# A fused two-mixer decoder layer: norm diagonals in a row, a doubling moved ahead, GELU's argument copied out of PSUM, and k gains applied behind the transposition

## The chip, the cores and the metric

The kernel runs on one core of one Trainium2 chip, as one launch. The metric is the device time of that launch in microseconds (us), the median of several runs. Inputs and outputs are float32.

The engines are named as in the profile: PE (TensorE, matmuls), DVE (VectorE), ACT (ScalarE), POOL (GpSimd) and SP (SyncE, which issues most DMAs). Every engine runs its instructions in the order in which they stand in the program; semaphores hold an instruction back until its operands are there and its buffer is free.

## The reference, cut to what matters

The layer takes x (1 x 512 x 1024), norms it, multiplies it by one wide input weight, and feeds two attention mixers of eight heads with 64 channels each. Mixer A (MoBA) is block-sparse attention; with 512 tokens and blocks of 256 its selection keeps every past block. Mixer B (NSA) has three branches: k and v compressed by a small MLP, selected blocks, and a window, the k of each branch with a gain vector of its own. The two outputs are gated, projected, merged and projected again.

```python
def rms_norm(x, g):
    y = xf * lax.rsqrt(jnp.mean(xf * xf, axis=-1, keepdims=True) + EPS)
    return y * g

def compress(kv, pos, w1, w2):          # windows of 32 tokens, stride 16
    win = kv[:, idx] + pos ...
    return jax.nn.gelu(win @ w1) @ w2

h = rms_norm(x, norm_w)
proj = h @ w_in
(q_a, k_a, v_a, z_a, q_b, kc, vc, ksl, vsl, kwn, vwn, gate_b, z_b, gate_m) = split(proj)
o_a = moba_mixer(rms_norm(q_a, q_norm_a), rms_norm(k_a, k_norm_a), v_a, bias_a)
k_cmp = rms_norm(compress(kc, ...), k_norm_cmp);  v_cmp = compress(vc, ...)
o_b = nsa_mixer(rms_norm(q_b, q_norm_b), k_cmp, v_cmp,
                rms_norm(ksl, k_norm_sel), vsl, rms_norm(kwn, k_norm_win), vwn, gate_b, bias_b)
merged = sigmoid(..) * ((o_a * silu(z_a)) @ w_branch_a) + sigmoid(..) * ((o_b * silu(z_b)) @ w_branch_b)
return x + merged @ w_out
```

## The kernel before, in words

**Float32 from three matmuls.** A float32 operand is split into a high part (rounded to fp32r) and a low part (the rest, again fp32r), and a product is hi·hi + lo·hi + hi·lo, all into one PSUM tile (`mm3`, L386). For a weight tile `wr` (128 x 512, from DRAM), ACT or POOL writes the high part `wh` (L352, L356) and DVE the low part `wl` (L361). A product over 1024 rows has eight such k tiles.

**A planner inside the kernel.** The kernel text holds streams of work (attention A, projections, compression, the norm of x) that yield to one another, and chains of small vector work. A chain's step is queued with `Chain.do(cost, f)`, where the cost names the engines that may do it and its length there in ns. While the program is built, the planner replays a modelled time `now`: it pops the chain step that is due first, puts it on the engine where it would end first, and books the cost. So the costs fix, at build time, the static order of each engine, and nothing is decided on the chip. A `do` whose function issues nothing still books its cost.

**Buffers.** PSUM tiles come from four groups: "g" (2 tiles, projections), "s" (2, scores), "t" (3, transpositions and small products), "o" (1, outputs). An instruction that writes a tile waits for the last reader of the tile that had the buffer before.

**The norm of x.** `rx` (128 x 4) is 1/rms for each token, token t·128 + p at (p, t). POOL makes it with a power (L513). It is used per token as a scale on copies out of PSUM (L718), and per column of a transposed product as a row R, the same in every partition. R is made on PE: `x_diag` (L519 to L531) splits `rx` into `rxh` (L523, POOL) and `rxl` (L524, DVE), multiplies the identity matrix with each (`dg`, L528, 128 x 512), and `x_rows` multiplies ones with the two `dg` into `prx` (L541). In this time PE runs the k tiles of `pgt` and `pgf`, projections; DVE also has the `v` tiles (L775) in its queue.

**q and k.** A projection of four heads comes out with tokens in partitions (`pgt`). `norm` (L709) copies it to `nraw` with the scale `rx` (L718, ACT), squares it (L720, ACT, with the later output tile as scratch), sums per head (L721, DVE), takes the power (POOL) and multiplies (L723). The gain vectors lie in `gn`, 6 x 64 floats repeated in all partitions; `norm` multiplies by q's and k's gain together where it can, on k alone. For mixer B's k, called `kb` (two groups with selected and window k each, 256 columns), that is L729, on DVE or POOL. `k_pair` (L969) then transposes 128 columns of four token tiles on PE into one PSUM tile `pq` (64 channels of one head in partitions 0 to 63, of the next in 64 to 127), and makes for each of the two heads `ks` (the high part twice, in partitions 0 to 63 and 64 to 127; L978, ACT) and `kx` (the low part in partitions 0 to 63, L980, DVE, and doubled into 64 to 127, L983, ACT). Mixer B's also leave `kf`, copies of the first 128 columns (L989). `q_pair` does the same for q: high part on top, low part below (`qs`, L963, L965).

**Attention.** A unit is one head. `qk` issues two matmuls per 128 queries into a score tile `sps`: `qs` with `ks` (L1024) and with `kx` (L1025). DVE adds the bias and finds the minimum in one custom instruction (`sb`, L1043, the last reader of `sps`), ACT exponentiates (L1058), POOL divides by the sum (L1062), PE transposes (`pt`, L1071), ACT and DVE split the result (`ph`, `pl`, L1083, L1085), and PE multiplies by v (L1105). `moba_units` has a `k_pair` for every second head, h = 0, 2, 4, 6, and `nsa_units` has two for `kb`.

**Compression.** `compress_h` (L852) multiplies windows with w1 into PSUM, copies the result to `hs` (L868, ACT), transposes it on PE into a PSUM tile `pu` (L873), and applies GELU in its tanh form: square on ACT (L878), times 0.044715 plus 1 on DVE (L879), times u on DVE (L880, u read from PSUM), tanh on ACT (L881), plus 1 and times u on DVE (L882, the last reader of `pu`). It runs once for k and once for v.

Of the kernel before, what the change touches and what calls it, by code (L numbers as in the profile page):

```python
# [106 lines left out]
def hybrid_kernel(ctx: ExitStack, tc: tile.TileContext, x, x0, xT, wtok, wchan, wz, wgate, gains, w1,  # L107
# [411 lines left out]
    def x_diag(c):  # L519
# [3 lines left out]
        c.do({"p": 160}, lambda e: e.tensor_scalar(rh, rx, 1.0, 1.0, op0=ALU.mult, op1=ALU.mult))  # L523
        c.do({"D": 70}, lambda e: e.tensor_sub(rl, rx, rh.bitcast(F32)))  # L524
        for r in (rh.bitcast(F32), rl):
            d = att("dg")
            dg.append(d)
            c.do(either(512), lambda e, r=r, d=d: e.tensor_mul(  # L528
                d.rearrange("p (t c) -> p t c", t=NT), ident.unsqueeze(1).to_broadcast([P, NT, P]),
                r.unsqueeze(2).to_broadcast([P, NT, P])))  # L530
# [178 lines left out]
    def norm(ch, dst, ps, t, H, gi):  # L709
# [14 lines left out]
        if gi == 1:  # L724
            z = out[:, 4:]
            ch.do(either(256), lambda e: e.tensor_mul(z, z, gn[:, 1, :].unsqueeze(1).to_broadcast([P, 4, DH])))
        elif gi:
# [1 line left out]
            ch.do(either(256), lambda e: e.tensor_mul(z, z, gn[:, gi:gi + 2, :].unsqueeze(2).to_broadcast([P, 2, 2, DH])))  # L729
# [120 lines left out]
    def compress_h(kv):  # L850
# [27 lines left out]
        ch.do({"A": 160}, lambda e: e.activation(t1, u, AF.Square))  # L878
# [90 lines left out]
    def k_pair(boxes, name, col, firsts=None):  # L969
# [5 lines left out]
        kk = [(att("ks"), att("kx")) for _ in range(2)]  # L975
        for r, (ks, kx) in enumerate(kk):
            for i in range(2):
                c.do({"A": 478}, lambda e, r=r, z=ks[64 * i:64 * i + 64, :]: e.copy(z, pt[64 * r:64 * r + 64, :]))  # L978
        for r, (ks, kx) in enumerate(kk):
            c.do({"D": 602}, lambda e, r=r, ks=ks, kx=kx: e.tensor_sub(  # L980
                kx[0:64, :], pt[64 * r:64 * r + 64, :], ks[0:64, :].bitcast(F32)), pt if r else None)
# [852 lines left out]
```

## Time and profile before

| | |
|---|---|
| median of 3 runs | 451.82 us (451.51 to 451.89) |
| the profiled execution's own time | 450.7 us |
| its span, first to last instruction | 448.9 us |
| granted TensorE clock, mean over the span | 0.999 |
| PE, busy | 441.9 us |
| DVE, busy | 383.2 us |
| ACT, busy | 302.8 us |
| POOL, busy | 199.9 us |

The span is 1.8 us shorter than the time of the same execution (450.7 − 448.9). Times in the profile count from the start of the span. In a row of a timeline the first number is the start, the second the duration, then come the engine, the line of the kernel, the operation and its tiles (out <- in) with their shapes; "x2" says that two like instructions in a row are taken together, and a bracket gives the idle time of the engine just before and who ended it. A row of the groups gives the count, then the busy time in all, the mean of one in ns, and behind a second bar the idle time before and its releaser. In a row of the waits stand who waited, for whom, the time in all, how many waits, and the longest.

### The profile page before, as it was taken

What the parts mean: (1) busy time and instruction counts of PE and PEld (TensorE: products, weight loads), DVE (VectorE), ACT (ScalarE), POOL (GpSimd) and SP (SyncE); (2) the same over time, 40 slices, a digit from 0 to 9 for tenths busy, and PEclk for the clock granted to TensorE, in tenths of its full rate; (3) what the DMA queues carried; (4) which work ended last, traced back from release to release, by engine and by line L of the source; (5) the groups of instructions that cost most, each with busy time, mean ns of one, the idle gap of its engine ahead of it and who ended that gap; (6) DMA issues with size and microseconds to landing.
All of it is one profiled execution on the core that took longest, in us unless ns stands there. A gap on an engine that the chain in (4) does not pass through costs nothing.

```text
span 448.9 us, 8538 instructions
## 1 busy us (share of the span) xinstructions
PE 441.9 (98%) x2779; PEld 394.0 (88%) x2779; DVE 383.2 (85%) x937; ACT 302.8 (67%) x711; POOL 199.9 (45%) x235
## 2 busy tenths in 40 slices
PE   8999999999999999999999999999999999999997
PEld 7878888899778999888999999989988999998886
DVE  5999899889997797788899899977967699899773
ACT  6866678867988798376877777687764355464450
POOL 1242337866685573177675654663770222211000
PEclk9999999999999999999999999999999999999999
DMA  8984655887975969859987867986667888889872
GB/s 252 300 269 166 245 157 180 206 244 197 265 200 164 216 208 279 287 142 220 245 239 203 220 189 170 249 221 159 194 179 174 241 227 249 243 239 295 283 235 95
DMA packets 55085, 98.21 MB, mean 219 GB/s; under 512 B 5312, under 2 KB 9536, under 8 KB 55040
## 3 DMA queue, kind: packets, MB, share of 16 engines
q1 hardware_dynamic: 39808, 68.30, 47.3%
q0 software_dynamic: 7616, 14.68, 20.3%
q10 hardware_dynamic: 7616, 14.68, 9.8%
q8 instruction: 22, 0.36, 0.3%
q14 instruction: 23, 0.19, 0.1%
HBM read 90.69 MB, written 36.31 MB: 283 GB/s over the span
## 4 chain that ended last, share of the span: by engine, by line
PE 79%; DVE 9%; ACT 7%; issue 2%; DMA 2%; POOL 0%; SPq 0%; ACTq 0%; DVEq 0%
PE pgw L386 19%; PE pgt L386 14%; PE pbr L386 10%; PE po L386 9%; PE pgc L386 7%; PE O L1105 6%; PE pt L1071 5%; PE sps L1024 3%; PE sps L1025 3%; DMA wr<-in_wtok 2%; DVE wl L361 1%; ACT ks L978 1%; DVE sb L1043 1%; DVE pl L1085 1%; PE pq L947 1%
## 5 line engine op out<-in xcount | busy, mean ns | idle before, releaser
L361 DVE TENSOR_TENSOR wl<-wr,wh 128x512 fp32r<-128x512 f32 (+1 forms) x150 | 103.5, 708 | 2.7 <-ACT wh L352 2.3
L352 ACT CAST wh<-wr 128x512 fp32r<-128x512 f32 (+1 forms) x130 | 76.7, 608 | 15.0 <-DMA wr<-wsum 6.5
L356 POOL TENSOR_SCALAR wh<-wr 128x512 fp32r<-128x512 f32 (+1 forms) x39 | 30.6, 794 | 79.2 <-DVE wl L361 20.9
L1062 POOL TENSOR_SCALAR P<-P,sst,gate 128x512 f32<-128x512 f32 (+3 forms) x56 | 46.7, 837 | 39.3 <-DVE sst L1061 31.3
L1058 ACT ACTIVATE P<-sb,sst 128x512 f32<-128x512 f32 (+3 forms) x88 | 50.7, 577 | 16.0 <-DVE sst L1043 14.6
L1043 DVE CUSTOM_DVE_ANT_0 sb<-sps,T 128x512 f32<-128x512 f32 (+3 forms) x96 | 46.0, 483 | 13.8 <-PE sps L1025 12.7
L386 PE MATMUL pgt<-wh,hh 128*128 128x512 f32 (+2 forms) x160 | 56.6, 354 | 0.0
L386 PE MATMUL pgt<-wl,hh 128*128 128x512 f32 (+2 forms) x160 | 55.9, 349 | 0.0
L386 PE MATMUL pgt<-wh,hl 128*128 128x512 f32 (+2 forms) x160 | 55.7, 348 | 0.0
L386 PE MATMUL pgw<-th,wh 128*128 128x256 f32 x240 | 48.8, 280 | 0.2 <-DVE gm L1519 0.2
L1083 ACT CAST ph<-pt 128x512 fp32r<-128x512 f32 (+2 forms) x72 | 33.8, 476 | 19.6 <-PE pt L1071 18.5
L386 PE MATMUL pgw<-hh,wh 128*128 128x256 f32 x160 | 45.1, 282 | 0.2 <-ACT c L1460 0.2
L386 PE MATMUL pgw<-hh,wl 128*128 128x256 f32 x160 | 44.4, 277 | 0.0
L386 PE MATMUL pgw<-hl,wh 128*128 128x256 f32 x160 | 44.4, 277 | 0.0
L1071 PE MATMUL pt<-cst,P 128*128 128x128 f32 x232 | 40.7, 272 | 0.3 <-DVE pl L1085 0.3
L1085 DVE TENSOR_TENSOR pl<-pt,ph 128x512 fp32r<-128x512 f32 (+2 forms) x72 | 38.7, 549 | 2.0 <-ACT ph L1083 1.8
L386 PEld LDWEIGHTS pgw<-th,wh 128*128 128x128 f32 x240 | 39.4, 188 | 0.8 <-DVE gm L1519 0.4
L427 POOL TENSOR_TENSOR nr<-nss,mhalf 128x8 f32<-128x8 f32 (+1 forms) x16 | 26.6, 1664 | 22.1 <-DVE nss L426 20.6
L386 PEld LDWEIGHTS pgt<-wl,hh 128*128 128x128 f32 x160 | 30.1, 188 | 4.4 <-DVE wl L361 0.4
L386 PE MATMUL pgw<-th,wl 128*128 128x256 f32 x120 | 33.3, 278 | 0.0
L386 PEld LDWEIGHTS pgt<-wh,hh 128*128 128x128 f32 x160 | 30.1, 188 | 3.4 <-ACT nraw L718 0.2
L386 PEld LDWEIGHTS pgt<-wh,hl 128*128 128x128 f32 x160 | 30.1, 188 | 3.3
(271 smaller groups left out, 1289.6 us busy)
## 6 DMA issues: line engine op xcount, KB each, us to landing
wr<-wsum SPq DMA_DIRECT2D x56, 256.0 KB, 3.8
wr<-in_wtok SPq DMA_DIRECT2D x36, 256.0 KB, 4.8
wsum<-in_wgate ACTq DMA_DIRECT2D x16, 512.0 KB, 5.3
wsum<-wsum POOLq DMA_DIRECT2D x14, 512.0 KB, 7.6
wr<-in_wgate SPq DMA_DIRECT2D x24, 256.0 KB, 4.8
xsum<-th SPq DMA_DIRECT2D x16, 256.0 KB, 2.4
T<-rtab SPq DMA_DIRECT2D x16, 256.0 KB, 5.3
wr<-in_w SPq DMA_DIRECT2D x16, 256.0 KB, 4.6
```

What stands on the lines that cost most here:

```text
L352: e.copy(hi, raw)
L356: e.tensor_scalar(hi, raw, 1.0, 1.0, op0=ALU.mult, op1=ALU.mult)
L361: c.do({"D": cd(n)} if lead else either(n), lambda e, hi=hi, lo=lo, raw=raw: e.tensor_sub(lo, raw, hi.bitcast(F32))).mark((w, 1, i))
L386: nc.tensor.matmul(dst, sts[i][a], mvs[i][b], start=(start and i == a == b == 0), stop=(stop and i == n - 1 and b == 1), skip_group_check= ...
L427: c.do({"p": 430 + POWC * w}, lambda e: e.tensor_tensor(v(dst), v(ss), mhalf[:parts, :w], op=ALU.pow))
L1043: e.tensor_tensor_reduce(z["sb"][:, :L], sps[:, :L], T[:, S - L:], scale=-1.0, scalar=3e38, op0=ALU.add, op1=ALU.min, accum_out=st[:, 0, b ...
L1058: e.activation(pv(), z["sb"][:, :L], AF.Exp, bias=st[:, 0, b:b + 1], scale=-1.0, accum_out=st[:, 1, b:b + 1])
L1062: c.do({"P": 315 + 0.834 * L}, lambda e: e.tensor_scalar(pv(), pv(), st[:, 2, b:b + 1], g, op0=ALU.mult, op1=ALU.mult))
L1071: nc.tensor.transpose(pt[:, (b - kb) * P:(b - kb + 1) * P], u.p0 if u.p0 is not None and b == 0 else u.pb[:, POFF[b] + kb * P:POFF[b] + (k ...
L1083: e.copy(z["w"][0], pt[:, :w])
L1085: ch.do({"D": cd(w)}, lambda e: e.tensor_sub(z["w"][1], pt[:, :w], z["w"][0].bitcast(F32)), pt)
L1105: nc.tensor.matmul(O[0][:, S - n:], v.bitcast(F32) if kb == 3 else v, w, start=(u.first and kb == 0 and i == 0), stop=(u.last and kb == 3 ...
```

## The change

Four edits; what PE computes, and the order of PE and of SP, are as before.

1. **Diagonals in a row.** In `x_diag`, `rxh` is a copy on DVE in place of a step on POOL, right ahead of `rxl`, and both `dg` multiplies are issued one behind the other. The costs that are no longer needed stay booked, with steps that issue nothing.
2. **k of mixer B weighted behind its transposition.** `norm` issues no gain multiply for `kb` (its cost stays booked). In `k_pair` for `kb` the four `ks` copies of a pair are an ACT activation Copy with a column of gains as scale, and the low part of `kx` is, on DVE, pq times the column minus `ks`. The columns (`gcol`: channel in partitions, one column per gain vector, the 64 channels twice) lie in the freed space of `gn`, whose array on the host is 128 x 262 in place of 384 floats; two of the four gain steps in `load_consts` work on 128 x 1 in place of 128 x 64.
3. **A doubling sooner.** In the `k_pair` of heads 4 and 5 of mixer A (h == 4), the doubling of the first `kx` is queued at once when its low part has been issued, not behind the low part of the second.
4. **GELU's argument copied.** In `compress_h`, ACT copies u from PSUM to SBUF right behind the square; the two steps in the middle go from DVE to POOL and read the copy, as does the last step on DVE.

```diff
@@ constants
+    gcol = gn[:, 4, :6]
@@ x_diag
-        c.do({"p": 160}, lambda e: e.tensor_scalar(rh, rx, 1.0, 1.0, op0=ALU.mult, op1=ALU.mult))
-        c.do({"D": 70}, lambda e: e.tensor_sub(rl, rx, rh.bitcast(F32)))
-        for r in (rh.bitcast(F32), rl):
...
-            c.do(either(512), lambda e, r=r, d=d: e.tensor_mul(
...
+        c.do({"p": 160}, lambda e: None)
+
+        def parts(e):
+            e.tensor_copy(rh, rx)
+            e.tensor_sub(rl, rx, rh.bitcast(F32))
+        c.do({"D": 70}, parts)
+
+        def diag(e):
+            for r, d in zip((rh.bitcast(F32), rl), dg):
+                e.tensor_mul(d.rearrange("p (t c) -> p t c", t=NT), ident.unsqueeze(1).to_broadcast([P, NT, P]),
+                             r.unsqueeze(2).to_broadcast([P, NT, P]))
+        dg.extend(att("dg") for _ in range(2))
+        c.do(either(512), diag).do(either(512), lambda e: None)
@@ norm
         elif gi:
-            z = out.rearrange("p (a b) d -> p a b d", a=2)
-            ch.do(either(256), lambda e: e.tensor_mul(z, z, gn[:, gi:gi + 2, :].unsqueeze(2).to_broadcast([P, 2, 2, DH])))
+            ch.do(either(256), lambda e: None)
@@ compress_h
-        u = ub[:, :P]
         t1 = sp.tile([P, P], F32, name=nm("gt"), tag="c2")
+        u = sp.tile([P, P], F32, name=nm("u"), tag="u", bufs=1)
         ch = Chain(now[0] + 230)
-        ch.do({"A": 160}, lambda e: e.activation(t1, u, AF.Square))
-        ch.do({"D": 200}, lambda e: e.tensor_scalar(t1, t1, 0.044715, 1.0, op0=ALU.mult, op1=ALU.add))
-        ch.do({"D": 200}, lambda e: e.tensor_mul(t1, t1, u))
+
+        def square(e):
+            e.activation(t1, ub[:, :P], AF.Square)
+            e.copy(u, ub[:, :P])
+        ch.do({"A": 160}, square)
+        ch.do({"D": 200}, lambda e: nc.gpsimd.tensor_scalar(t1, t1, 0.044715, 1.0, op0=ALU.mult, op1=ALU.add))
+        ch.do({"D": 200}, lambda e: nc.gpsimd.tensor_mul(t1, t1, u))
@@ k_pair
-    def k_pair(boxes, name, col, firsts=None):
+    def k_pair(boxes, name, col, firsts=None, gi=None, sooner=False):
...
+        def double():
+            nc.scalar.copy(kk[0][1][64:128, :], kk[0][1][0:64, :].bitcast(F32))
+
+        def high(e, r, z):
+            if gi is None:
+                e.copy(z, pt[64 * r:64 * r + 64, :])
+            else:
+                e.activation(z, pt[64 * r:64 * r + 64, :], AF.Copy, scale=gcol[64 * r:64 * r + 64, gi:gi + 1])
+
+        def low(e, r, ks, kx):
+            z = pt[64 * r:64 * r + 64, :], ks[0:64, :].bitcast(F32)
+            if gi is None:
+                e.tensor_sub(kx[0:64, :], *z)
+            else:
+                e.scalar_tensor_tensor(kx[0:64, :], z[0], gcol[64 * r:64 * r + 64, gi:gi + 1], z[1], op0=ALU.mult, op1=ALU.subtract)
+            if sooner and not r:
+                Chain(now[0] + KX0).call(double)
...
-            c.do({"A": ca(512)}, lambda e, kx=kx: e.copy(kx[64:128, :], kx[0:64, :].bitcast(F32)))
+            c.do({"A": ca(512)}, lambda e, r=r, kx=kx: (r or not sooner) and e.copy(kx[64:128, :], kx[0:64, :].bitcast(F32)))
@@ moba_units, nsa_units
-                    yield from k_pair(ks, f"qk{h // 4}", 256 + h % 4 * DH)
+                    yield from k_pair(ks, f"qk{h // 4}", 256 + h % 4 * DH, sooner=h == 4)
...
-                    yield from k_pair(kbox, "kb", P * br, [z[:, :, br, :] for z in both])
+                    yield from k_pair(kbox, "kb", P * br, [z[:, :, br, :] for z in both], gi=4 + br)
```

The edits move instructions on DVE, ACT and POOL. VectorE's order where the norm of x is made, before; `pss` is the sum of squares, `wr`, `wh` and `wl` are weight tiles, `rt` belongs to the bias table:

```order
L512 TENSOR_SCALAR rx_93<-pss69_375 128x4
L361 TENSOR_TENSOR wl67_366<-wr63_355,wh66_365 128x512
L799 COPY rt79_396<-pR80_397 128x512
L524 TENSOR_TENSOR rxl_393<-rx_93,rxh_392 128x4
L361 TENSOR_TENSOR wl84_418<-wr68_371,wh83_417 128x512
L528 TENSOR_TENSOR dg77_394<-cst_94,rxh_392 128x512
L361 TENSOR_TENSOR wl86_420<-wr70_380,wh85_419 128x512
L528 TENSOR_TENSOR dg78_395<-cst_94,rxl_393 128x512
L775 SCALAR_TENSOR_TENSOR v088_442<-pgf21_172,rx_93,v088_442 128x4x64
```

The same place with the change:

```order
L514 TENSOR_SCALAR rx_93<-pss69_375 128x4
L362 TENSOR_TENSOR wl67_366<-wr63_355,wh66_365 128x512
L805 COPY rt79_396<-pR80_397 128x512
L528 CAST rxh_392<-rx_93 128x4
L529 TENSOR_TENSOR rxl_393<-rx_93,rxh_392 128x4
L362 TENSOR_TENSOR wl84_418<-wr68_371,wh83_417 128x512
L534 TENSOR_TENSOR dg77_394<-cst_94,rxh_392 128x512
L534 TENSOR_TENSOR dg78_395<-cst_94,rxl_393 128x512
L362 TENSOR_TENSOR wl86_420<-wr70_380,wh85_419 128x512
```

The second `dg` has moved ahead of one weight's low part, and `rxh` has come to VectorE.

ScalarE's order where the compression of k meets the last projection of `kb` and the k pair of heads 4 and 5, before; `kx385` and `kx387` are that pair's low parts, `gt` is GELU's tile, `nraw` and `kb` belong to the norm:

```order
L718 ACTIVATE nraw405_1697<-pgt391_1614,rx_93 128x256
L352 CAST wh410_1706<-wr382_1601 128x512
L878 ACTIVATE gt409_1705<-pu408_1701 128x128
L720 ACTIVATE kb401_1672<-nraw405_1697 128x256
L352 CAST wh412_1716<-wr397_1649 128x512
L983 CAST kx385_1607<-kx385_1607 64x512
L983 CAST kx387_1609<-kx387_1609 64x512
L881 ACTIVATE gt409_1705<-gt409_1705 128x128
```

The same place with the change (L988 is the doubling that is queued sooner, L1010 the other):

```order
L725 ACTIVATE nraw405_1695<-pgt391_1614,rx_93 128x256
L988 CAST kx385_1607<-kx385_1607 64x512
L353 CAST wh411_1706<-wr382_1601 128x512
L886 ACTIVATE gt409_1704<-pu408_1700 128x128
L887 COPY u410_1705<-pu408_1700 128x128
L727 ACTIVATE kb401_1671<-nraw405_1695 128x256
L353 CAST wh413_1717<-wr397_1648 128x512
L1010 CAST kx387_1609<-kx387_1609 64x512
L891 ACTIVATE gt409_1704<-gt409_1704 128x128
```

One doubling has moved up by four instructions, and the copy of u stands behind the square.

VectorE's order at that place, before (`nss` is the norm's sum, `sb` the scores with bias):

```order
L980 TENSOR_TENSOR kx387_1609<-pq381_1586,ks386_1608 64x512
L879 TENSOR_SCALAR gt409_1705<-gt409_1705 128x128
L721 TENSOR_REDUCE nss406_1698<-kb401_1672 128x4
L880 TENSOR_TENSOR gt409_1705<-gt409_1705,pu408_1701 128x128
L723 TENSOR_TENSOR kb390_1613<-nraw394_1638,nr396_1640 128x256
L426 TENSOR_SCALAR nss406_1698<-nss406_1698 128x4
L361 TENSOR_TENSOR wl413_1717<-wr397_1649,wh412_1716 128x512
L729 TENSOR_TENSOR kb390_1613<-kb390_1613,gn_95 128x256
L882 SCALAR_TENSOR_TENSOR gt409_1705<-gt409_1705,pu408_1701 128x128
L1043 ISA sb419_1750,sst416_1742<-sps415_1737,T388_1610 128x512
```

The same place with the change:

```order
L999 TENSOR_TENSOR kx387_1609<-pq381_1586,ks386_1608 64x512
L728 TENSOR_REDUCE nss406_1696<-kb401_1671 128x4
L730 TENSOR_TENSOR kb390_1613<-nraw394_1637,nr396_1639 128x256
L428 TENSOR_SCALAR nss406_1696<-nss406_1696 128x4
L362 TENSOR_TENSOR wl414_1718<-wr397_1648,wh413_1717 128x512
L892 SCALAR_TENSOR_TENSOR gt409_1704<-gt409_1704,u410_1705 128x128
L1070 ISA sb420_1749,sst417_1741<-sps416_1736,T388_1610 128x512
```

Two GELU steps and the gain multiply of `kb` are gone from VectorE; the two GELU steps now stand on POOL.

More of the change, by code (lines that the diff above doesn't have):

```diff
@@ L57 @@
 POWC = 180
+KX0 = 0
 CMARGIN = 1000
@@ L522, in x_diag @@
         rh, rl = (cp.tile([P, NT], dt_, name=n_) for n_, dt_ in (("rxh", F32R), ("rxl", F32)))
-        c.do({"p": 160}, lambda e: e.tensor_scalar(rh, rx, 1.0, 1.0, op0=ALU.mult, op1=ALU.mult))
-        c.do({"D": 70}, lambda e: e.tensor_sub(rl, rx, rh.bitcast(F32)))
-        for r in (rh.bitcast(F32), rl):
[L526 to L530, printed above, removed]
+        c.do({"p": 160}, lambda e: None)
[9 more added lines that the diff above has]
+        c.do(either(512), diag).do(either(512), lambda e: None)
         c.mark("dg")
@@ L975, in k_pair @@
         kk = [(att("ks"), att("kx")) for _ in range(2)]
+        def double():
[13 more added lines that the diff above has]
+                Chain(now[0] + KX0).call(double)
         for r, (ks, kx) in enumerate(kk):
             for i in range(2):
-                c.do({"A": 478}, lambda e, r=r, z=ks[64 * i:64 * i + 64, :]: e.copy(z, pt[64 * r:64 * r + 64, :]))
+                c.do({"A": 478}, lambda e, r=r, z=ks[64 * i:64 * i + 64, :]: high(e, r, z))
         for r, (ks, kx) in enumerate(kk):
-            c.do({"D": 602}, lambda e, r=r, ks=ks, kx=kx: e.tensor_sub(
-                kx[0:64, :], pt[64 * r:64 * r + 64, :], ks[0:64, :].bitcast(F32)), pt if r else None)
+            c.do({"D": 602}, lambda e, r=r, ks=ks, kx=kx: low(e, r, ks, kx), pt if r else None)
         for r, (ks, kx) in enumerate(kk):
-            c.do({"A": ca(512)}, lambda e, kx=kx: e.copy(kx[64:128, :], kx[0:64, :].bitcast(F32)))
+            c.do({"A": ca(512)}, lambda e, r=r, kx=kx: (r or not sooner) and e.copy(kx[64:128, :], kx[0:64, :].bitcast(F32)))
             for i, z in enumerate((ks, kx) if firsts else ()):
@@ L1549, in load_consts @@
         c.do({"P": 547}, lambda e: e.tensor_copy(identr, ident)).mark("ident")
-        dma(gn, bass.AP(tensor=gains.tensor, offset=gains.offset, ap=[[0, P], [1, 6 * DH]]), 1536)
+        dma(gn.rearrange("p k d -> p (k d)")[:, :4 * DH + 6], gains, 1536)
         o = alloc("P", "oh", (64, TW))
@@ L1559, in load_consts @@
         for i, k in ((0, 1), (2, 3), (2, 4), (2, 5)):
-            c.do({"D": 102}, lambda e, i=i, k=k: e.scalar_tensor_tensor(gn[:, k, :], gn[:, i, :], 0.125, gn[:, k, :], op0=ALU.mult,
-                                                                        op1=ALU.mult))
+            z = (lambda n: gn[:, n, :]) if k < 4 else (lambda n: gcol[:, n:n + 1])
+            c.do({"D": 102}, lambda e, z=z, i=i, k=k: e.scalar_tensor_tensor(z(k), z(i), 0.125, z(k), op0=ALU.mult, op1=ALU.mult))
     def gemms():
@@ L1796, in _layout @@
     gains = np.concatenate([f[k][0] for k in ("q_norm_a", "k_norm_a", "q_norm_b", "k_norm_cmp",
-                                               "k_norm_sel", "k_norm_win")])
+                                               "k_norm_sel", "k_norm_win")]).reshape(6, DH)
+    gains = np.concatenate([np.tile(gains[:4].reshape(1, -1), (P, 1)), np.tile(gains.T, (2, 1))], 1)
     posT = np.stack([f[k][0].reshape(16, 2, DH).transpose(1, 2, 0).reshape(P, 16)
```

## The prediction, made before the change was run

> **What bounds the kernel now.** First the page: TensorE's share of the span.
>
> ```profile
> span 448.9 us, 8538 instructions
> PE 441.9 (98%) x2779; PEld 394.0 (88%) x2779; DVE 383.2 (85%) x937; ACT 302.8 (67%) x711; POOL 199.9 (45%) x235
> ```
>
> TensorE sets the time. So an edit elsewhere counts only as far as it moves a moment at which TensorE waits. Next, the list of who waited for whom, TensorE's rows; the columns are microseconds in all, times, longest.
>
> ```profile
> PE sps L1025 <- ACT kx L983: 1.0, 1, 1.0
> PE prx L541 <- DVE dg L528: 0.7, 1, 0.7
> ```
>
> These two waits lie where the change lies; a third, smaller one shows in place three. Such a wait is counted from the modelled end of the matmul before; the chain of work gives the true pace:
>
> ```profile
> 31.42 20.48 PE pgt L386 x90
> ```
>
> 90 matmuls of 128x512 in 20.48 us are 0.23 us each, start to start. The three places follow, in order of time.
>
> **Place one, 25 to 35 us: the norm's diagonal matrices.** The timeline of VectorE, then of GpSimd, then of TensorE (start, duration):
>
> ```profile
> 27.44 0.16 DVE L524 TENSOR_TENSOR rxl<-rx,rxh 128x4 f32<-128x4 f32 x1 [0.79 <-POOL rxh L523]
> 27.52 0.69 DVE L361 TENSOR_TENSOR wl<-wr,wh 128x512 fp32r<-128x512 f32 x1
> 28.13 0.69 DVE L528 TENSOR_TENSOR dg<-cst,rxh 128x512 fp32r<-128x512 f32 x1
> 28.73 1.10 DVE L361 TENSOR_TENSOR wl<-wr,wh 128x512 fp32r<-128x512 f32 x1
> 29.76 1.10 DVE L528 TENSOR_TENSOR dg<-cst,rxl 128x512 fp32r<-128x512 f32 x1
> 30.78 3.21 DVE L775 SCALAR_TENSOR_TENSOR v<-pgf,rx,v 128x256 fp32r<-128x256 f32 x8
> ...
> 34.25 0.68 DVE L361 TENSOR_TENSOR wl<-wr,wh 128x512 fp32r<-128x512 f32 x1
> ```
>
> ```profile
> 25.54 1.42 POOL L513 TENSOR_TENSOR rx<-rx,mhalf 128x4 f32<-128x4 f32 x1 [1.89 <-DVE rx L512]
> ...
> 28.51 1.82 POOL L356 TENSOR_SCALAR wh<-wr 128x512 fp32r<-128x512 f32 x2 [1.10 <-PE pgf L675]
> ```
>
> ```profile
> 29.80 0.39 PE L541 MATMUL prx<-dg,ones 128*128 128x512 f32 x1
> 30.92 0.50 PE L541 MATMUL prx<-dg,ones 128*128 128x512 f32 x1 [0.72 <-DVE dg L528]
> ...
> 35.18 0.39 PE L386 MATMUL pgt<-wl,hh 128*128 128x512 f32 x1
> ```
>
> The second `prx` matmul starts 1.12 us behind the first; at 0.23 that is a stall of 0.89 us. It ends when the second `dg` is made, and between the two `dg` stands a weight's low part. The change puts the high part of the norm on VectorE (rx is there at 25.54 + 1.42 = 26.96, so about 27.0), takes GpSimd's step out, and makes both `dg` before that low part. Two tiny steps of 0.16, the second waiting for the first, put the low part ahead of them at about 27.26 where it was 27.52; and two of the four gain steps that run before rx shrink from 64 columns to one:
>
> ```profile
> L1560 DVE SCALAR_TENSOR_TENSOR gn<-gn 128x64 f32<-128x64 f32 x4 | 0.9, 214 | 0.0
> ```
>
> I take 0.1 for both (each loses between nothing and its 0.21). The second `dg` then starts at 27.15 + 0.61 + 0.60 = 28.36, just ahead of GpSimd's 28.51, and is done between 29.05 (0.69 as the first one, which GpSimd also found running) and 29.46 (1.10). TensorE wants it at 29.80 + 0.23 = 30.03. The stall goes in either case: −0.89.
>
> What is late next is the low part at 34.25, the last k tile of the running product. It ends at 34.93 and TensorE takes it at 35.18; 0.89 earlier is 34.29. VectorE reaches the `v` block at 30.78 now. After the change the second `dg` and the low part behind it come to 28.36 + 0.60 + 1.03 = 30.0 if only one of the two is slowed, 30.4 if both are: 0.78 or 0.38 sooner. The last low part ends at 34.15 or 34.55, so TensorE waits nothing or 0.3. I take 0.85 as the gain, because the `dg` that started before GpSimd took 0.69 in the row above; the ends are 0.25 (VectorE no sooner) and 1.0 (the sum's 0.89 and a shorter restart). [...]
>
> **Place two, 119 to 126 us: the doubled low part and compression's GELU.** ScalarE, then VectorE, then TensorE:
>
> ```profile
> 119.80 0.47 ACT L718 ACTIVATE nraw<-pgt,rx 128x256 f32<-128x256 f32 x1
> 120.16 0.61 ACT L352 CAST wh<-wr 128x512 fp32r<-128x512 f32 x1
> 120.67 0.28 ACT L878 ACTIVATE gt<-pu 128x128 f32<-128x128 f32 x1
> 120.84 0.42 ACT L720 ACTIVATE kb<-nraw 128x256 f32<-128x256 f32 x1
> 121.15 0.62 ACT L352 CAST wh<-wr 128x512 fp32r<-128x512 f32 x1
> 121.79 1.14 ACT L983 CAST kx<-kx 64x512 fp32r<-64x512 f32 x2
> 122.95 0.31 ACT L881 ACTIVATE gt<-gt 128x128 f32<-128x128 f32 x1
> ```
>
> ```profile
> 123.39 0.28 DVE L882 SCALAR_TENSOR_TENSOR gt<-gt,pu 128x128 f32<-128x128 f32 x1
> 123.59 0.68 DVE L1043 CUSTOM_DVE_ANT_0 sb<-sps,T 128x512 f32<-128x512 f32 x1
> ...
> 124.19 1.04 DVE L361 TENSOR_TENSOR wl<-wr,wh 128x512 fp32r<-128x512 f32 x1
> ```
>
> ```profile
> 122.46 0.50 PE L1025 MATMUL sps<-kx,qs 128*128 128x512 f32 x1 [0.96 <-ACT kx L983]
> ...
> 124.33 0.38 PE L1024 MATMUL sps<-ks,qs 128*128 128x256 f32 x1
> ...
> 125.29 0.50 PE L386 MATMUL pgt<-wl,hh 128*128 128x512 f32 x1
> ```
>
> The change puts the first `kx` doubling right behind `nraw`: done at 120.9, so the matmul of 122.46 runs some 1.1 us sooner. But the score tile of 124.33 is the third, and two PSUM buffers hold scores: it starts when VectorE has read the first (`sb`, 123.59 + 0.68 = 124.27). `sb` stands behind GELU's last step on VectorE, and that waits for ScalarE's tanh at 122.95. So the wait moves to 124.33 and nothing is gained there, unless tanh comes sooner. It comes later. ScalarE is occupied without a break from 119.80, and stepping through its new order with the starts above: `nraw` 119.80, `kx` 120.30 (an op ahead of a doubling takes its full time: 0.64 from 121.15 to 121.79, where its like took 0.51), weight 120.94, square 121.45, copy of u 121.62 (as the square, 0.17), `kb` 121.79, weight 122.10, second `kx` 122.74, tanh 123.37. That is 0.42 later: 0.17 for the copy, the rest for parting the two doublings. VectorE's last step goes to 123.37 + 0.34 = 123.71, `sb` to 123.91 to 124.59, the score tile to 124.65: 0.32 late. The low part behind `sb` is then done at 125.2 to 125.55, and the matmul of 125.29 starts at 125.46 to 125.6. Place two costs +0.3.
>
> The two GELU steps that go to GpSimd run beside ScalarE's 121.7 to 123.4 if they are short. No row shows them; the nearest:
>
> ```profile
> L989 POOL TENSOR_SCALAR kf<-kx 128x128 fp32r<-128x128 f32 x1 | 0.3, 295 | 0.0
> L729 POOL TENSOR_TENSOR kb<-kb,gn 128x256 f32<-128x256 f32 x2 | 1.9, 925 | 1.1 <-DVE kb L723 1.0
> ```
>
> 0.3 for the first, and for the second at most the 0.93 of a tile twice as wide: 121.82 to 123.1, in time. If both take 0.93 tanh is 0.35 later still. Bounds of place two: −0.1 (second half of the restart goes) to +0.7. The multiply by gains that goes from VectorE and GpSimd lies beside this and is worth nothing: what follows it there waits for ScalarE.
>
> **Place three, 154 to 175 us: k weighted behind its transposition.** ScalarE in this stretch, from the table of stages (after the two stage lengths come PE, PEld, DVE, ACT, POOL), and its two kinds of read from PSUM, plain and with a column as scale:
>
> ```profile
> 154.60:172.90 18.30, 18.30 (x152) 18.03 (x152) 13.40 (x35) 17.91 (x43) 9.41 (x12) 1.00 0.79 225
> ```
>
> ```profile
> L1083 ACT CAST ph<-pt 128x512 fp32r<-128x512 f32 x24 | 14.0, 585 | 17.1 <-PE pt L1071 16.9
> L978 ACT CAST ks<-pq 64x512 fp32r<-64x512 f32 x24 | 13.9, 580 | 0.4
> L718 ACT ACTIVATE nraw<-pgt,rx 128x512 f32<-128x512 f32 x12 | 8.2, 687 | 8.3 <-PE pgt L386 8.1
> ```
>
> A scale from a column costs 687 − 585 = 102 ns at this width. Eight `ks` copies get one, all between 156 and 172 us, where ScalarE is busy 17.91 of 18.30 us. At the end of that stretch VectorE and TensorE wait for it:
>
> ```profile
> 172.87 0.69 DVE L965 TENSOR_TENSOR qs<-pq,qs 64x512 fp32r<-64x512 f32 x1
> 173.56 0.69 DVE L980 TENSOR_TENSOR kx<-pq,ks 64x512 fp32r<-64x512 f32 x1
> ```
>
> ```profile
> 174.41 0.63 PE L873 MATMUL pu<-cst,hs 128*128 128x64 f32 x4 [0.24 <-DVE kx L980]
> ```
>
> `pu` needs the PSUM buffer that `kx` reads last; `kx` is queued behind `qs`, which needs ScalarE's last copies. So 8 × 0.102 = 0.82 arrives whole. `kx` itself becomes a scalar_tensor_tensor: two `v` steps of 256 columns take 2 × 0.40 by the row at 30.78, `kx` 0.69, so +0.1 at most; I take 0.05. Place three: +0.87, between 0 (ScalarE's delay is covered) and 1.0. A gain is excluded: nothing leaves ScalarE. [...]
>
> Second GELU (175 to 180): its matmuls stand behind work with spare time; zero.
>
> **The sum.** −0.85 + 0.30 + 0.87 = +0.32 us on the profiled run's 450.7, 451.0. That run lies 1.1 under the median of 451.82, so 452.1 by the median. No change is what a measurement of this kernel cannot tell from 0.2%, 0.9 us.
>
> **Rivals.** *The first gain is handed back* (slower): at 34.25 the last k tile's low part is no earlier, because both `dg` and the step behind them are slowed by GpSimd. For: both 1.10 rows. Against: two steps leave the queue ahead. It decides once the `v` block starts later than 30.6: gain 0.25, sum −0.25 + 0.30 + 0.87 = +0.92, 452.7. *The wait for kx is real*: the third score tile is free in time, so 1.1 goes at place two: −0.85 − 1.1 + 0.87 = −1.08, 450.7. For: the wait list. Against: 123.59 + 0.68 against 124.33. *The weighted copies are covered*: TensorE would have spare work to 175: −0.85 + 0.30 = −0.55, 451.3. Against: it already waits 0.24 there. *All three waits go* (0.89 + 1.12 + 0.4): 449.4.
>
> **Chances.** Forecast 0.50 (its own range 451.5 to 452.9); handed back 0.20; kx real 0.12; copies covered 0.12; all go 0.06. Faster by over 0.2%: 0.12 + 0.06 = 0.18. Slower: half of the handed-back case, 0.10 (its +0.92 lies on the bound), and the forecast's upper end, 0.08: 0.18. Within: 0.64. The range takes the kx case at its lower end, 450.7, and above the handed-back case with place three's upper bound, 453.0; "all go" and tails stay out.
>
> **What would show it.** Right: no wait of `prx`; the low part near 34.2; a new TensorE wait of over 1 us at the third score tile, for VectorE's `sb`, in place of that for `kx`; tanh some 0.4 later against `nraw`; `ks` at 0.68; `pu` waiting over 1 us. Wrong: `sps` of the third tile without a wait, `pu` no later than now, or a GpSimd step of GELU over 1 us.

## The result, and the profile after

The changed kernel takes 454.01 us (median of 6 runs, 452.56 to 455.09) against 451.43 us (6 runs, 450.63 to 451.89): 1.0056 times as long, 95% interval 1.0041 to 1.0072. That is 2.6 us slower; the forecast was 452.1 us and its range ended at 453.0.

The page of the changed kernel: span and busy times. Then TensorE's longest waits.

```profile
span 452.4 us, 8534 instructions
PE 444.6 (98%) x2779; PEld 396.4 (88%) x2779; DVE 381.7 (84%) x932; ACT 304.4 (67%) x713; POOL 196.5 (43%) x236
```

```profile
PE sps L1051 <- DVE sst L1070: 1.5, 1, 1.5
PE pu L879 <- DVE kx L1001: 1.0, 1, 1.0
```

The waits for `dg` and for `kx` are gone. In their place stand one of 1.5 us at the third score tile, and one of 1.0 us at `pu` where it was 0.24.

The order of TensorE is the same in both kernels, so each of its matmuls can be set against itself. The table gives its start in a profile minus its start in the profile of before (us; plus is late), for the first matmul at or behind the given time of before; the one behind 124.5 is the second of the third score tile. The other rows are the experiments below; the run with the made pauses, which has other matmuls, is left out.

| | 28 | 34 | 112 | 124.5 | 128 | 154 | 176 | 440 |
|---|---|---|---|---|---|---|---|---|
| changed kernel | +0.27 | −0.79 | −0.41 | +0.05 | +1.69 | +1.60 | +3.07 | +3.47 |
| diagonals alone | +0.13 | −0.93 | −0.20 | −0.22 | −0.20 | −0.28 | −0.28 | +1.60 |
| weighting alone | +0.17 | −0.40 | −0.02 | −0.10 | 0.00 | −0.07 | +1.39 | +2.37 |
| doubling sooner alone | +0.41 | −0.27 | +0.03 | +0.72 | +2.29 | +2.21 | +2.21 | +4.82 |
| GELU's copy alone | +0.08 | −0.33 | +0.29 | +0.68 | +0.41 | +0.33 | +0.34 | +0.56 |
| changed, pause filled | −0.33 | −1.37 | +0.17 | +0.62 | +0.68 | +0.69 | +2.15 | +2.74 |
| before, doubling twice | +0.40 | −0.05 | +0.57 | +1.14 | +0.88 | +0.81 | +0.80 | +1.25 |
| before, doubling three times | +0.41 | −0.03 | +0.53 | +1.73 | +1.45 | +1.45 | +1.43 | +1.85 |
| sb first | +0.25 | −0.81 | −0.56 | −1.05 | +0.17 | +0.07 | +0.07 | +0.45 |
| sb first, GELU last | +0.15 | −0.91 | −0.35 | −0.83 | −0.69 | −0.29 | −0.27 | +0.55 |
| weighting, plain ks | +0.48 | −0.51 | −0.65 | −0.75 | −0.65 | −0.65 | −0.55 | −0.09 |
| changed, plain ks | −0.20 | −1.26 | −0.51 | −0.03 | +0.04 | −0.03 | +0.07 | +0.31 |

Three steps make the changed kernel's row: a gain around 30 us, partly given back by 112 us; 0.46 us at the third score tile and 1.64 us right behind it; and 1.47 us between 154 and 176 us. The 1.64 us belongs to no wait. From 176 to 440 us every row falls back by 0.2 to 2.6 us, though behind 182 us VectorE, ScalarE and GpSimd have the same order as before: single executions differ by as much, and the profile of before is a quick one (450.7 us against the median of 451.43).

**Place one.** VectorE, GpSimd and TensorE in the changed kernel:

```profile
27.13 0.69 DVE L362 TENSOR_TENSOR wl<-wr,wh 128x512 fp32r<-128x512 f32 x1
27.74 0.69 DVE L534 TENSOR_TENSOR dg<-cst,rxh 128x512 fp32r<-128x512 f32 x1
28.34 0.69 DVE L534 TENSOR_TENSOR dg<-cst,rxl 128x512 fp32r<-128x512 f32 x1
...
33.16 0.68 DVE L362 TENSOR_TENSOR wl<-wr,wh 128x512 fp32r<-128x512 f32 x1
```

```profile
29.46 1.24 POOL L357 TENSOR_SCALAR wh<-wr 128x512 fp32r<-128x512 f32 x2 [2.35 <-DMA wr<-in_wchan]
```

```profile
30.07 0.62 PE L548 MATMUL prx<-dg,ones 128*128 128x512 f32 x2
```

The second `dg` starts at 28.34 and takes 0.69, the two `prx` run without a stall, and the last low part is 1.09 us sooner (34.25 before).

**Place two.** ScalarE, VectorE, GpSimd, TensorE:

```profile
119.38 0.48 ACT L725 ACTIVATE nraw<-pgt,rx 128x256 f32<-128x256 f32 x1
119.88 0.62 ACT L988 CAST kx<-kx 64x512 fp32r<-64x512 f32 x1
...
122.97 0.31 ACT L891 ACTIVATE gt<-gt 128x128 f32<-128x128 f32 x1
```

```profile
123.31 0.29 DVE L892 SCALAR_TENSOR_TENSOR gt<-gt,u 128x128 f32<-128x128 f32 x1
123.63 0.69 DVE L1070 CUSTOM_DVE_ANT_0 sb<-sps,T 128x512 f32<-128x512 f32 x1
```

```profile
121.42 0.29 POOL L889 TENSOR_SCALAR gt<-gt 128x128 f32<-128x128 f32 x1 [0.32 <-ACT gt L886]
121.80 0.47 POOL L890 TENSOR_TENSOR gt<-gt,u 128x128 f32<-128x128 f32 x1
```

```profile
122.27 0.60 PE L957 MATMUL pq<-cst,qk 128*128 128x128 f32 x4
124.38 0.39 PE L1051 MATMUL sps<-ks,qs 128*128 128x256 f32 x1 [1.51 <-DVE sst L1070]
```

From `nraw` to tanh it is 3.59 us, where it was 3.15; the wait has moved from `kx` to `sb`, and has grown from 0.96 to 1.51 us. The table of stages right behind it, cut at 3.41 us (after the two stage lengths: PE, PEld, DVE, ACT, POOL, then the granted clock):

```profile
122.49:125.91 3.42, 1.85 (x10) 1.14 (x9) 3.33 (x10) 2.48 (x7) 1.99 (x2) 1.00 0.76 256
125.91:129.32 3.41, 3.41 (x10) 2.32 (x9) 2.48 (x9) 2.86 (x8) 1.91 (x4) 0.50 0.79 255
```

For 3.41 us TensorE has half its clock: half the work of that stretch, 1.7 us of it, comes late.

**Place three.** The scaled copies and the scaled low parts in the changed kernel's groups:

```profile
L994 ACT ACTIVATE ks<-pq,gn 64x512 fp32r<-64x512 f32 x8 | 5.4, 681 | 0.1
L1001 DVE SCALAR_TENSOR_TENSOR kx<-pq,gn,ks 64x512 fp32r<-64x512 f32 x4 | 3.0, 748 | 0.9 <-ACT ks L994 0.9
```

101 ns more for a `ks` (580 before), 0.06 us more for a low part (0.69).

### The profile page after: what moved, and what is told of

Same layout as the page of the kernel before. It is cut to its first block, busy times and chain, and to the rows that moved or that the text cites. A ratio compares the mean times of both kernels' runs of the same rounds, so it can differ in the third digit from the quotient of the medians.

```text
span 452.4 us, 8534 instructions
## 1 busy us (share of the span) xinstructions
PE 444.6 (98%) x2779; PEld 396.4 (88%) x2779; DVE 381.7 (84%) x932; ACT 304.4 (67%) x713; POOL 196.5 (43%) x236
## 4 chain that ended last, share of the span: by engine, by line
PE 86%; DVE 7%; ACT 5%; issue 2%; POOL 0%; ACTq 0%; POOLq 0%
PE pgw L387 19%; PE pgt L387 14%; PE pbr L387 10%; PE po L387 8%; PE pgc L387 7%; PE O L1132 6%; PE pt L1098 5%; PE pgf L682 5%; PE sps L1051 3%; PE sps L1052 3%; DVE sb L1070 1%; PE pq L957 1%; ACT ks L994 1%; DVE pl L1112 1%; DVE vl L362 1%
## 5 line engine op out<-in xcount | busy, mean ns | idle before, releaser
L357 POOL TENSOR_SCALAR wh<-wr 128x512 fp32r<-128x512 f32 (+1 forms) x39 | 28.6, 742 | 81.0 <-DVE wl L362 35.0
L1098 PEld LDWEIGHTS pt<-cst,P 128*128 128x128 f32 x232 | 29.2, 141 | 4.8 <-PE pgw L387 0.5
```

The lines of the kernel that those rows point to most:

```text
L357: e.tensor_scalar(hi, raw, 1.0, 1.0, op0=ALU.mult, op1=ALU.mult)
L1098: nc.tensor.transpose(pt[:, (b - kb) * P:(b - kb + 1) * P], u.p0 if u.p0 is not None and b == 0 else u.pb[:, POFF[b] + kb * P:POFF[b] + (k ...
```

## The experiments

Each edit is shown short. A time is set against runs of the kernel before on the same chip in the same session.

**The four edits, each alone on the kernel before** (their diffs are those of the change).

> The kernel before with the diagonals in a row alone. Theory A (what the two traces show, term by term): the stall of 0.89 us in prx goes, TensorE is 1.0 us early at 34 us, a third of it is given back by 111 us where VectorE meets GpSimd's weight steps, and the time falls by 0.6 to 0.8 us. Theory B (the gain of this place is handed back wholly, as the rival of the prediction had it): TensorE is level by 111 us and the time the same.

451.06 us against 451.35: 0.9989, 0.9974 to 1.0004, which does not exclude that nothing changed. In the table TensorE gains 1.06 us between 28 and 34 us, in this and in each of the other five profiles with the new diagonals 1.04 to 1.06. But the other six, which have the old ones, pass the same place 0.41 to 0.99 us sooner than the profile of before as well. The weighting alone, VectorE and TensorE:

```profile
29.40 1.10 DVE L530 TENSOR_TENSOR dg<-cst,rxl 128x512 fp32r<-128x512 f32 x1
```

```profile
30.56 0.50 PE L543 MATMUL prx<-dg,ones 128*128 128x512 f32 x1 [0.20 <-DVE dg L530]
```

The second `dg` takes 1.10 as in the profile of before, but starts 0.36 us sooner, and TensorE waits 0.20 where it waited 0.72. What sets the profile of before apart is GpSimd's first weight step: it came at 28.51 there, ahead of the low part of 28.73, and both that low part and the second `dg` took 1.10. In the other seven profiles with the old order it came at 28.80 to 29.33, within 0.02 us of that low part's start or behind it; the low part took 0.69, and only the second `dg` 1.10. From 28 to 112 us the six with the new diagonals come to −0.81 to +0.50, median −0.42, the six with the old ones to −1.13 to +0.21, median −0.04. The two sets overlap, so that the edit's worth there, some 0.4 us, is a rough size.

> The kernel before with mixer B's k weighted behind the transposition alone. Theory A: ScalarE falls back by 0.8 us from the eight scaled copies and some 0.3 to 0.5 us from steps that this parts, pu waits 0.9 us or more, and the time rises by 1.0 to 1.4 us with the granted clock at 0.999. Theory B (TensorE had spare work there and only the lateness from further ahead makes the wait): pu waits 0.24 us as before and the time rises by less than 0.3 us.

452.82 us against 451.35: 1.0031, 1.0017 to 1.0046, so +1.47. TensorE loses 0.70 us between 163 and 172 us, and more at `pu`: 1.46 us in all from 154 to 176 (the changed kernel 1.47). ScalarE ahead of it, before and with the weighting alone:

```profile
156.25 1.16 ACT L978 CAST ks<-pq 64x512 fp32r<-64x512 f32 x2
157.43 0.58 ACT L1130 COPY ot<-O 64x512 f32<-64x512 f32 x1
157.91 0.58 ACT L978 CAST ks<-pq 64x512 fp32r<-64x512 f32 x1
...
171.85 0.37 ACT L768 ACTIVATE vb<-pgt,rx 128x128 fp32r<-128x128 f32 x1
```

```profile
156.18 1.36 ACT L985 ACTIVATE ks<-pq,gn 64x512 fp32r<-64x512 f32 x2
157.56 0.58 ACT L1148 COPY ot<-O 64x512 f32<-64x512 f32 x1
158.17 0.69 ACT L985 ACTIVATE ks<-pq,gn 64x512 fp32r<-64x512 f32 x1
...
166.77 0.37 ACT L769 ACTIVATE vb<-pgt,rx 128x128 fp32r<-128x128 f32 x1 [0.27 <-DVE vb L770]
...
173.16 0.37 ACT L769 ACTIVATE vb<-pgt,rx 128x128 fp32r<-128x128 f32 x1
```

The stretch begins 0.07 us sooner and its last row is 1.31 us late: 1.38 us more. 0.81 of it is the copies' own length (8 × 0.101). 0.27 is a wait for VectorE that was not there. The rest lies in the spacing; in the rows shown a plain `ks` starts 0.48 behind the start of `ot`, a scaled one 0.61 behind it.

> The kernel with the weighting of k alone, but with the high parts ks copied plainly, so that the gains are left out of them (the low parts still take their column): one edit apart from the run with the weighting alone. Theory A (the eight scaled copies on ScalarE are the cost): 1.0 to 1.3 us of that run's 1.47 go, pu waits 0.2 to 0.4 us, and the time is within 0.4 us of the kernel before. Theory B (the cost is VectorE's low part with a column, or the order that the missing multiply leaves): the time stays at 452.5 or above.

```diff
         def high(e, r, z):
-            if gi is None:
-                e.copy(z, pt[64 * r:64 * r + 64, :])
-            else:
-                e.activation(z, pt[64 * r:64 * r + 64, :], AF.Copy, scale=gcol[64 * r:64 * r + 64, gi:gi + 1])
+            e.copy(z, pt[64 * r:64 * r + 64, :])
```

451.18 us against 451.14: 1.0000, 0.9985 to 1.0015; TensorE loses 0.10 us between 154 and 176. TensorE's wait in the run with the weighting alone, then in this one:

```profile
PE pu L874 <- DVE kx L992: 1.0, 1, 1.0
```

```profile
PE pu L874 <- DVE kx L989: 0.3, 1, 0.3
```

The whole cost of place three comes from the eight scaled copies, with what they set off behind them. The low parts with a column and the missing multiply cost no more than the 0.10 us that are left between 154 and 176.

> The kernel before with the first doubling sooner alone. Theory A (the wait moves to the third score tile, and a pause of over about 1.2 us in one piece brings the granted clock down): the wait for kx goes, the third score tile waits 1.1 to 1.4 us for VectorE's sb, TensorE is 0 to 0.3 us late behind it; if its clock then falls to a half for 3 to 4 us, the time rises by 1.5 to 1.8 us, else by 0 to 0.3. Theory B (the fall of the clock is an event of chance that has nothing to do with the pause): clock 0.999 and the time the same within 0.3 us. Theory C (the forecast's rival, the wait for kx is real): the time falls by 1 us.

452.79 us against 451.35: 1.0032, 1.0016 to 1.0048. The wait is not where any theory had it. TensorE, and VectorE:

```profile
124.53 0.63 PE L949 MATMUL pq<-cst,qk 128*128 128x128 f32 x4 [1.66 <-DVE gt L884]
```

```profile
124.11 0.28 DVE L884 SCALAR_TENSOR_TENSOR gt<-gt,pu 128x128 f32<-128x128 f32 x1
```

The transpositions `pq` need the PSUM buffer of `pu`, which GELU's last step reads here. The copy of u lifts that in the whole change, so the two edits belong together. The clock falls behind this pause too, from 126.10 to 129.51 us (mean of that profile 0.996).

> The kernel before with GELU's argument copied out of PSUM and the two middle steps on GpSimd alone. Theory A: the copy adds 0.17 us ahead of both doublings, the wait for kx grows by 0.17 us and the third score tile does not wait; the time rises by 0.2 us, the clock stays. Theory B (the copy brings no delay since ScalarE catches up): same within 0.1 us. If GpSimd's two steps held tanh up, the third score tile would wait as well.

451.31 us against 451.35: 1.0001, 0.9988 to 1.0013. The wait for `kx` is 1.16 us (0.96 before); the 0.2 us is too small for the times to show.

**The fall of the clock.** In each profile the clock changes only at times that lie whole multiples of 3.413 us apart (in the changed kernel it rises at 6.44 and falls at 125.91, 119.47 us or 35 steps later). The first rise lay between 3.54 and 6.76 us in 14 profiles, spread over nearly a full step: the grid's place differs from execution to execution.

> The kernel before with a made pause of TensorE ahead of each of the 14 groups of q and k transpositions: a transposition, 2 to 13 short copies of it on ScalarE one behind the other, and a transposition that reads the last copy (the result is overwritten by the real ones). Pauses of about 1 to 3.5 us at 14 places of one execution. Theory W (the clock is set anew on a fixed grid of 3.41 us, whose phase differs from execution to execution, and falls to a half for a step when TensorE was idle for more than some 1.4 to 1.6 us within one step): every fall begins on the grid, every grid step with idle time over one threshold is followed by a fall, and none under it; pauses of 1.5 to 2.5 us that a grid line parts bring none. Theory L (the length of the pause alone decides): all pauses over one length bring a fall, beginning at a fixed time behind them. The time rises by some 20 to 35 us.

```diff
+        nc.tensor.transpose(pt[:, :P], toks[name][0][:, col:col + P], ident)
+        for _ in range(PAUSE.pop(0)):
+            nc.scalar.copy(scr, pt[:, :P])
+        nc.tensor.transpose(pt[:, :P], scr, ident)
         for t in range(NT):
             nc.tensor.transpose(pt[:, t * P:(t + 1) * P], toks[name][t][:, col:col + P], ident)
```

501.83 us; ScalarE's queue made the pauses longer than meant (TensorE's 14 waits for the copies come to 36.0 us, the longest 4.8; the falls of the clock below took 12.0), hence the 50 us. Two steps of its grid, each with the next one:

```profile
60.84:64.25 3.41, 1.59 (x10) 1.41 (x11) 1.97 (x5) 2.86 (x10) 1.26 (x2) 1.00 0.14 49
64.25:67.66 3.41, 3.41 (x17) 2.80 (x16) 2.56 (x5) 3.29 (x7) 0.65 (x2) 1.00 0.53 154
77.91:81.33 3.42, 1.55 (x12) 1.24 (x11) 1.18 (x5) 3.33 (x11) 1.80 (x3) 1.00 0.23 86
81.33:84.74 3.41, 3.41 (x11) 2.74 (x10) 1.78 (x9) 2.41 (x8) 0.58 (x1) 0.50 0.79 199
```

Modelled ends blur the busy column: a matmul of 512 columns stands there with 0.39 us where the next one starts 0.227 behind it. I counted each matmul at what its like takes back to back: 0.227 us for 512 columns and in proportion (0.114 for 256), 0.11 for a transposition of 128. Then some 1800 steps at full clock of 14 profiles (without the last of each, where the work ends) part cleanly: the 8 that a fall followed had TensorE working 0.03 to 0.39 of the step, and all others 0.45 or more (the pairs above: 0.45, no fall; 0.39, a fall). Theory W holds, with a share of work for the threshold, between 0.39 and 0.45, rather than one pause's length.

> The kernel before, with the doubling for which TensorE waits issued twice (the same values again), so that its wait for kx grows from 1.0 to about 1.5 us, all else as before. Theory A: the clock falls to a half behind it as in the changed kernel, and the time rises by 0.5 + 1.5 = 2.0 us. If only pauses of over 1.5 us do that, by 0.5 us with the clock at 0.999. Theory B (no link with the pause): 0.5 us.

> The same with the doubling issued three times: the wait grows to about 2.1 us. Theory A: the clock falls to a half for 3 to 4 us, the time rises by 1.1 + 1.5 = 2.6 us. Theory B: by 1.1 us, clock 0.999.

```diff
-            c.do({"A": ca(512)}, lambda e, kx=kx: e.copy(kx[64:128, :], kx[0:64, :].bitcast(F32)))
+            c.do({"A": ca(512)}, lambda e, r=r, kx=kx: [e.copy(kx[64:128, :], kx[0:64, :].bitcast(F32)) for _ in range(2 if long and not r else 1)])
```

Twice: 451.91 us against 451.25, 1.0010, 0.9997 to 1.0023. Three times: 452.66, 1.0031, 1.0014 to 1.0049. The second one's profile has the longest pause of all but the made ones, and no fall; TensorE, and two steps of its grid:

```profile
124.27 0.50 PE L1025 MATMUL sps<-kx,qs 128*128 128x512 f32 x1 [2.26 <-ACT kx L983]
```

```profile
120.25:123.67 3.42, 1.76 (x8) 1.10 (x6) 3.30 (x11) 3.33 (x9) 2.07 (x3) 1.00 1.06 218
123.67:127.08 3.41, 2.81 (x19) 2.59 (x20) 2.28 (x8) 3.12 (x7) 2.19 (x3) 1.00 0.79 249
```

A grid line at 123.67 parts the pause; the worst step keeps a share of 0.46. So theory A of these two, with the length alone, falls. Every timed run lists its mean clock, and one fall takes 0.5 × 3.41 us of some 450, so a run with a fall shows 0.995 or 0.996, others 0.999 or 1.000. Beside the count stands the share of grid places at which some step between 110 and 132 us would have less work than about 0.41, an estimate worked out from the profile:

| | share of grid places | runs with a fall | median without / with (us) |
|---|---|---|---|
| changed kernel | 0.24 | 2 of 6 | 453.40 / 454.63 |
| doubling sooner alone | 0.26 | 4 of 12 | 452.50 / 454.09 |
| before, doubling three times | 0.56 | 6 of 12 | 451.73 / 453.28 |
| changed, plain ks | 0.25 | 3 of 12 | 451.00 / 454.11 |
| before, doubling twice | 0.00 (lowest 0.44) | 1 of 12 | 451.89 / 452.80 |
| changed, pause filled | 0.00 | 0 of 6 | 453.76 / – |
| six others (all but the pauses at 14 places) | 0.00 | 0 of 72 | |
| before, beside the last experiment | 0.00 | 1 of 17 | 451.64 / 455.10 |

The threshold is known only to lie between 0.39 and 0.45. Over that span the changed kernel's share goes from 0.15 to 0.43, and at 0.45 the doubling issued twice has 0.35, so its one fall is no exception; the counts agree with the shares and do not fix them. The one fall of the kernel before is not explained by its profile's pauses; in its other lists of 35, 29 and 23 runs there is none.

> The changed kernel, with the four transpositions ahead of the third score tile's matmul issued three more times, into the same PSUM tile with the same values (1.3 us of TensorE work that changes nothing, inside the pause of 1.5 us). Theory A (the pause brings TensorE's clock down to a half for 3 to 4 us): the third score tile starts when it did, the pause shrinks to 0.2 to 0.4 us, the granted clock stays at 1.00 between 124 and 131 us, and the time falls by 1.0 to 1.5 us against the changed kernel, to 452.5 to 453.0. Theory B (the clock falls by chance or from load): the time stays at the changed kernel's 454.0, and the clock falls here too.

```diff
+        if (name, col) == ("qk1", 2 * DH):
+            for t in 3 * list(range(NT)):
+                nc.tensor.transpose(pt[:, t * P:(t + 1) * P], toks[name][t][:, col:col + P], ident)
```

453.76 us against 451.25: 1.0066, 1.0047 to 1.0085. The pause shrinks to 0.20 us, the clock stays in all six runs, and in the profile TensorE loses 0.06 us from 124.5 to 128 where the changed kernel lost 1.64. The time did not come down, though, and part of it lies at place one, which has the changed kernel's order here. VectorE, GpSimd and TensorE:

```profile
28.39 1.11 DVE L534 TENSOR_TENSOR dg<-cst,rxl 128x512 fp32r<-128x512 f32 x1
29.42 1.10 DVE L362 TENSOR_TENSOR wl<-wr,wh 128x512 fp32r<-128x512 f32 x1
30.44 3.21 DVE L781 SCALAR_TENSOR_TENSOR v<-pgf,rx,v 128x256 fp32r<-128x256 f32 x8
```

```profile
28.33 1.64 POOL L357 TENSOR_SCALAR wh<-wr 128x512 fp32r<-128x512 f32 x2 [1.19 <-PE pgf L682]
```

```profile
34.64 0.51 PE L387 MATMUL pgt<-wl,hh 128*128 128x512 f32 x1 [0.27 <-DVE wl L362]
```

GpSimd's first weight step came at 28.33 here, just ahead of the second `dg`, and at 29.46 in the changed kernel's profile. The second `dg` and the low part behind it take 1.1 us each, and TensorE's lead goes from 1.37 us at 34 to 0.41 at 36. The stall at the last low part is the rival "handed back", in this execution. The clock at 128 us is shown; a gain in the median is not.

> The changed kernel with the high parts ks copied plainly (the gains are left out of them), all its other edits in place: what is left is the diagonals' row and place two. Theory W (terms add: diagonals -0.3 us, the moved wait +0.5 us, and a fall of the clock that costs 1.6 us in the executions whose 3.41 us grid lies so that one step holds the whole pause, a quarter to a half of them): TensorE neither loses nor gains between 154 and 176 us, and the median lies 0.6 to 1.0 us above the kernel before, at 451.8 to 452.3, with single times up to 453.5 or more. Theory B (the clock plays no part in the medians): 0.2 us above, 451.4. Theory C (place three costs through lateness from place two as well): TensorE loses 0.4 us or more between 154 and 176 us.

The edit of the plain `ks`, on the changed kernel. 451.64 us against 451.69: 1.0007, 0.9983 to 1.0030, −0.8 to +1.4 us, an interval that holds theory W's 0.6 to 1.0 us and no change at all. Three of twelve runs have a fall (453.62, 454.11, 454.57), the other nine end at 452.14 or below. TensorE gains and loses nothing between 154 and 176 (+0.10), so theory C falls: place three costs by itself. With the scaled copies gone the 2.6 us are gone too, within this interval; what place two costs is read from the traces and from the runs with a fall, not from this median. The profile caught no fall, with the same pause:

```profile
124.30 0.39 PE L1048 MATMUL sps<-ks,qs 128*128 128x256 f32 x1 [1.55 <-DVE sst L1067]
```

```profile
121.44:124.85 3.41, 1.86 (x14) 1.57 (x13) 3.02 (x8) 3.12 (x7) 2.64 (x4) 1.00 0.69 204
124.85:128.27 3.42, 3.37 (x18) 2.17 (x16) 3.32 (x12) 2.67 (x9) 0.95 (x2) 1.00 0.85 238
```

**A better order at place two.** The other three edits without the weighting, and by hand on VectorE: one weight's low part (`HOLD`), `kb`'s gain multiply and GELU's last step are kept back while the order is built, and issued behind `sb` and the next weight's low part (`FREE`):

```diff
+                def low(e, hi, lo, raw, k):
+                    if k == HOLD:
+                        return late.append(lambda: e.tensor_sub(lo, raw, hi.bitcast(F32)))
+                    e.tensor_sub(lo, raw, hi.bitcast(F32))
+                    while k == FREE and late:
+                        late.pop(0)()
```

> The kernel before with the diagonals in a row, the doubling sooner and GELU's argument copied, without the weighting of k, and with VectorE's order turned at the third score tile: the scores with bias (sb) ahead of a weight's low part, of a gain multiply and of GELU's last step. Theory A (the third score tile waits for sb because sb stands behind steps that wait for ScalarE): that wait shrinks from 1.5 to 0.3 to 0.6 us, the clock stays, TensorE is 0.8 to 1.0 us earlier behind it than in the kernel before; with the diagonals' 0.3 to 0.5 us the time falls by 1.1 to 1.5 us, to about 450.0. Rival (the weight's low part that was moved behind becomes late): a wait for wl of 0.3 to 0.8 us instead, and the time falls by 0.3 to 0.8 us.

451.62 us against 451.25: 1.0012, 1.0001 to 1.0022. The third score tile starts 1.05 us sooner than in before, and 1.2 us are lost by 128 us. TensorE, and VectorE:

```profile
127.16 0.41 PE L1112 MATMUL pt<-cst,P 128*128 128x128 f32 x2 [1.05 <-DVE pl L1126]
```

```profile
123.75 1.10 DVE L367 TENSOR_TENSOR wl<-wr,wh 128x512 fp32r<-128x512 f32 x1
124.78 0.95 DVE L749 TENSOR_TENSOR kb<-kb,gn 128x256 f32<-128x256 f32 x1
...
126.33 1.14 DVE L1126 TENSOR_TENSOR pl<-pt,ph 128x512 fp32r<-128x512 f32 x2
```

The steps that were put behind `sb` now stand ahead of `pl`.

> As the run with VectorE's order turned, but with GELU's last step and the gain multiply moved behind the low parts of the transposed probabilities (pl) too. Theory (pl was late by 1.1 us there because these two steps stood ahead of it): the wait of the transpositions for pl falls from 1.1 us to 0.2 to 0.5 us, the time falls to 450.5 to 451.0, below both kernels by 0.3 us or more against the one before. Rival (place two cannot give anything, since VectorE has no spare time between 121 and 128 us): the same as with the other order, 451.6, a wait for pl, sb or pk of the same size.

```diff
+                ch.do({"D": cd(w)}, lambda e: (e.tensor_sub(z["w"][1], pt[:, :w], z["w"][0].bitcast(F32)), flush()), pt)
```

GELU's last step and the multiply are now held until both `pl` are issued (`flush`). 450.88 us against 451.14: 0.9988, 0.9976 to 1.0000. The wait for `pl` is gone and TensorE is 0.48 us sooner from 112 to 124.5 and 0.34 from 112 to 128, but by 154 us nothing is left (−0.29 against −0.35). What remains is about the gain of the diagonals. This is the fastest of the versions, below the kernel before by no more than can just be told.

## Why the prediction was wrong

- **Place one, −0.85: right mechanism, size half.** The second `dg` was forecast at 28.36 and came at 28.34, at 0.69 as chosen. That was luck in part: GpSimd came at 29.46, not at 28.51, behind the start of both it and the low part that follows (28.94), which took 0.69 and 0.68, so the last low part came sooner than forecast. The step that failed is the stall of 0.89 us from one execution: in six others with the same order TensorE passed that place 0.41 to 0.99 us sooner. By 112 us the edit is worth about 0.4 us, and alone it measures 0.3, not told from none.
- **Place two, +0.30: the wait as forecast, its consequence not.** The wait moved to the third score tile for `sb` behind tanh, tanh came 0.44 us later against `nraw` (0.42 forecast), GpSimd's steps took 0.29 and 0.47 us. The loss at that tile is 0.46 us from 112 to 124.5. The sum priced the pause by the lateness at its end alone. It did not have a term for the clock, which fell to 0.50 for 3.41 us behind a step of the grid with 0.39 of work or less: 1.2 to 3.1 us between the medians with and without, in a quarter to a half of the runs with such a pause. In the profile of before no such fall lay behind its pause of 0.96 us.
- **Place three, +0.87: right mechanism, size too small.** A scaled `ks` costs 101 ns more (102 forecast). The step "8 × 0.102 arrives whole" took ScalarE's delay for the copies' own length; 1.47 us arrived, since ScalarE, busy 17.91 of 18.30 us there, also passed on wider spacing (0.61 us behind the start of `ot` where it was 0.48) and a new wait of 0.27 us for VectorE.
- **The sum.** −0.3 and +1.47 measured alone, +0.46 for the moved wait, and a third of the runs with 1.6 us more, 0.5: 2.1 us, against 2.6 with an interval of 1.9 to 3.3. The 0.5 is a mean over runs, and the means of the changed kernel and of the one before differ by 2.4. What is left is within the interval and is not put down to anything.
- **Rivals.** The first gain handed back: in the run with the pause filled, by its own mechanism, though with the `v` block at 30.44, earlier than the 30.6 of its sign; not in the changed kernel's profile. Its 452.7 is the nearest of them, but not for its reason. That `kx` is a real wait falls with the 1.51 us at the next tile; even with `sb` first the place gives nothing that lasts. The covered copies fall with the 1.47 us.
